# Masked softmax on one core: small writes to the output placed beside the first whole loads

## The chip, the cores and the metric

The kernel runs on one core of a Trainium2 chip. The metric is the device time of one execution in microseconds (us). The kernel before takes 156.7 us.

## The reference

```python
x: (16, 8, 256, 256) float32;  lengths: (16,) int32, 128 to 255
for b in range(16):
    length = lengths[b]
    m = x[b, :, :, :length]
    m = exp(m - max(m, axis=-1))
    result[b, :, :, :length] = m / sum(m, axis=-1)      # the rest of the row is 0
```

## The kernel before

Each of the 16 batch entries is one tile of 2 MB: 128 partitions, 16 rows of 256 floats each. SP's queue loads the first four tiles whole (the first in two halves) and later stores all sixteen. GpSimd loads the other twelve, only as wide as the length requires ("gap loads" in the prediction). VectorE masks a tile, ScalarE takes Exp row by row with the row sum, VectorE divides, SP stores. The output of the last tile is written at the very end.

```python
nc.scalar.dma_start(out=word64, in_=lengths[None, :]).then_inc(s_word, 16)
for h in range(2):                                     # tile 0 in two halves
    s = slice(h * half, (h + 1) * half)
    nc.sync.dma_start(out=xt[:, 0, s], in_=x_f[0, :, s]).then_inc(s_ld[h], 16)
for b in range(1, ahead):                              # tiles 1 to 3, whole
    nc.sync.dma_start(out=xt[:, b], in_=x_f[b]).then_inc(s_ld[b + 1], 16)
for b in range(batch):                                 # all stores
    for s in parts(b):
        nc.sync.wait_ge(s_out, 2 * b + (s.stop - 1) // half + 1)
        ...
        nc.sync.dma_start(out=out_f[b, :, s, :], in_=xt[:, b % slots, s, :]).then_inc(s_b, ...)
...
nc.gpsimd.wait_ge(s_ld[ahead - 1], 16)                 # GpSimd's loads begin after tile 2
with nc.Fori(0, (batch - ahead) // 2, 1, engines=[POOL]) as q:
    ...                                                # one narrow load for each later tile
...
nc.scalar.activation(out=warm, ...)                    # loads the Exp table
with nc.Fori(0, 2 * batch, 1, engines=[ACT]) as i:     # 8 Exp with row sums per half tile
    nc.scalar.wait_ge(s_min, i + 1)
    ...
```

The softmax here doesn't subtract the row's maximum and nothing guards it: scores larger than these inputs give would overflow.

Of the kernel before, what the change touches and what calls it, by code (L numbers as in the profile page):

```python
# [9 lines left out]
F32 = mybir.dt.float32  # L10
# [10 lines left out]
def kernel(  # L21
# [6 lines left out]
    nc = tc.nc  # L28
    P = nc.NUM_PARTITIONS

    batch, heads, seq_q, seq_k = x.shape
# [7 lines left out]
    out_f = out.rearrange("b h q k -> b (h q) k").rearrange("b (p t) k -> b p t k", p=P)  # L39
# [10 lines left out]
    def parts(b):  # L50


        if b == 0:
            cuts = [0, nt]
        elif b < 10:
            cuts = [0, half, half + quarter, nt]
        elif b < 12 or b == batch - 1:
            cuts = [0, half, nt]
        else:
            cuts = [0, nt]  # L60
        return [slice(i, j) for i, j in zip(cuts, cuts[1:])]

    pool = ctx.enter_context(tc.tile_pool(name="all", bufs=1))
# [10 lines left out]
    row_sum = pool.tile([P, batch, nt], F32, name="row_sum")  # L74
    inv_sum = pool.tile([P, batch, nt], F32, name="inv_sum")
    warm = pool.tile([P, 1], F32, name="warm")
    seed = pool.tile([1, 2], F32, name="seed")

    with tc.tile_critical(no_gpsimd_drain=True):  # L79
        sem = lambda n: ctx.enter_context(nc.semaphore(n))  # L80
        s_word = sem("s_word")
        s_ones = sem("s_ones")
        s_lenb = sem("s_lenb")
        s_lenf = sem("s_lenf")
        s_ld = [sem(f"s_ld{k}") for k in range(ahead + 1)]
# [18 lines left out]


        nc.scalar.dma_start(out=word64, in_=lengths[None, :]).then_inc(s_word, 16)
        for h in range(2):
            s = slice(h * half, (h + 1) * half)
            nc.sync.dma_start(out=xt[:, 0, s], in_=x_f[0, :, s]).then_inc(s_ld[h], 16)  # L109
        for b in range(1, ahead):  # L110
            nc.sync.dma_start(out=xt[:, b], in_=x_f[b]).then_inc(s_ld[b + 1], 16)  # L111
        for b in range(batch):
            s_b = s_st[b % 2]
            for s in parts(b):
                nc.sync.wait_ge(s_out, 2 * b + (s.stop - 1) // half + 1)
                if b >= 2 and s.start == 0:
                    nc.sync.wait_ge(s_b, 64 * (b // 2 + 1))
                nc.sync.dma_start(  # L118
                    out=out_f[b, :, s, :], in_=xt[:, b % slots, s, :]
                ).then_inc(s_b, 16 * ((s.stop - s.start) // quarter))  # L120
# [49 lines left out]
        def step(ins):  # L170
# [8 lines left out]
                out=down, in0=iota_i, scalar1=0.5, scalar2=-big, op0=ALU.add, op1=ALU.mult  # L179
# [7 lines left out]
                out=len_s, in0=len_f, scalar1=big, scalar2=None, op0=ALU.mult  # L187
# [56 lines left out]
        with nc.Fori(0, 2 * batch, 1, engines=[ACT]) as i:  # L244
            nc.scalar.wait_ge(s_min, i + 1)
            at = bass.ds(i % (2 * slots), 1)
            for j in range(half):
                e = x_h[:, at, j, :]
                ins = nc.scalar.activation(  # L249
                    out=e, in_=e, func=EXP, accum_out=sum_h[:, bass.ds(i, 1), j]  # L250
# [32 lines left out]
```

## Time and profile before

| | before |
|---|---|
| device time | 156.71 us median (156.7 to 157.01, 3 runs) |
| span in the profile | 154.7 us |
| busiest compute engine | VectorE, 115.1 us |
| queue shares of the DMA engines | 66.1% + 32.1% |
| stretch with a low rate | 20 to 24 us |

The span ends when the last store has landed. As the DMA engines are busy for nearly all of it, a change in this kernel is worth what it adds to or takes from their time. The prediction shows the lines and reads them.

The trace also has one record for each DMA packet, with its queue, size, start and duration. The usual duration of a packet, from the medians that the prediction gives, is 7 ns plus its bytes at 27.1 bytes per ns. A packet is called slow when it took over 1.25 times that. The "excess" of a stretch is the slow packets' time above the usual, of SP's and ScalarE's large packets (4 KB and more), summed and divided by 16 engines. By this count the kernel before has 0.96 us of excess from 19 to 24 us, and 0.60 us in the first 5 us; in the rest of the execution it has 0.03 us. (The prediction summed over all packets of the first stretch, not only the slow ones, and so has 1.1 us.)

### The profile page before, as it was taken

What the parts mean: (1) busy time and instruction counts of PE and PEld (TensorE: products, weight loads), DVE (VectorE), ACT (ScalarE), POOL (GpSimd) and SP (SyncE); (2) the same over time, 40 slices, a digit from 0 to 9 for tenths busy, and PEclk for the clock granted to TensorE, in tenths of its full rate; (3) what the DMA queues carried; (4) which work ended last, traced back from release to release, by engine and by line L of the source; (5) the groups of instructions that cost most, each with busy time, mean ns of one, the idle gap of its engine ahead of it and who ended that gap; (6) DMA issues with size and microseconds to landing.
All of it is one profiled execution on the core that took longest, in us unless ns stands there. A gap on an engine that the chain in (4) does not pass through costs nothing.

```text
span 154.7 us, 1317 instructions
## 1 busy us (share of the span) xinstructions
PE 0.2 (0%) x1; PEld 0.1 (0%) x1; DVE 115.1 (74%) x84; ACT 105.2 (68%) x514; POOL 19.0 (12%) x25
## 2 busy tenths in 40 slices
PE   0000000000000000000000000000000000000000
PEld 0000000000000000000000000000000000000000
DVE  1249999952999994966979499999894999990000
ACT  3087799992698997591978849798969297920000
POOL 4910031000320200202020020202000000000000
DMA  4999999999999999999999999999999999999993
GB/s 108 430 445 424 436 309 416 409 411 436 423 404 388 423 405 416 412 412 422 398 421 412 411 413 404 414 409 412 417 409 450 417 420 426 443 432 436 424 415 144
DMA packets 10132, 62.08 MB, mean 401 GB/s; under 512 B 866, under 2 KB 962, under 8 KB 6802
## 3 DMA queue, kind: packets, MB, share of 16 engines
q1 hardware_dynamic: 6048, 41.95, 66.1%
q0 software_dynamic: 4080, 20.12, 32.1%
q14 instruction: 2, 0.02, 0.0%
q10 hardware_dynamic: 2, 0.00, 0.0%
HBM read 28.51 MB, written 33.55 MB: 401 GB/s over the span
## 4 chain that ended last, share of the span: by engine, by line
DMA 71%; DVE 12%; issue 4%; POOLq 1%; SPq 1%; DVEq 0%
DMA xt<-in_x_dram 60%; DMA out_dram<-xt 11%; DVE xt L222 9%; DVE xt L195 3%; SPq L109 1%; POOLq L135 1%; DVE inv_sum L219 0%; POOLq L130 0%; SPq L111 0%; SPq L118 0%; POOLq L157 0%; POOLq L159 0%; DVEq L212 0%; POOLq L137 0%; SPq L278 0%
## 5 line engine op out<-in xcount | busy, mean ns | idle before, releaser
L249 ACT ACTIVATE xt<-xt x256 | 102.4, 402 | 29.6 <-DVE xt L195 29.6
L222 DVE TENSOR_TENSOR xt<-xt,inv_sum 128x2048 f32<-128x2048 f32 x32 | 73.3, 2292 | 1.1
L195 DVE SCALAR_TENSOR_TENSOR xt<-down,len_s,xt 128x2048 f32<-128x2048 f32 (+1 forms) x17 | 37.8, 2224 | 19.8 <-DMA xt<-in_x_dram 19.4
L249 ACT ACTIVATION_READ_ACCUMULATOR xt<-xt x256 | 48.1, 188 | 0.0
L130 POOL DMA_DIRECT2D xt<-in_x_dram x12 | 12.8, 1066 | 91.3 <-DMA out_dram<-xt 62.8
L219 DVE RECIPROCAL inv_sum<-row_sum 128x8 f32<-128x8 f32 x32 | 6.3, 196 | 1.2 <-ACT xt L249 1.2
L149 POOL MEMSET xt<- 128x1536 f32 x4 | 5.3, 1387 | 1.1 <-DVE len_s L186 1.1
L241 ACT ACT_TABLE_LOAD x1 | 1.3, 1283 | 1.6 <-SPq L79 1.6
L178 DVE TENSOR_SCALAR down<-iota_i 128x256 f32<-128x256 int32 x1 | 0.3, 299 | 1.6 <-POOL iota_i L141 1.6
L183 DVE CAST len_b<-word 1x16 bf16<-1x16 int32 x1 | 0.2, 162 | 0.4 <-DMA word<-in_lengths_dram 0.4
L186 DVE TENSOR_SCALAR len_s<-len_f 128x16 f32<-128x16 f32 x1 | 0.2, 175 | 0.3 <-PE len_f L165 0.3
L141 POOL IOTA iota_i<- 128x256 int32 x1 | 0.3, 332 | 0.6 <-SPq L79 0.6
L146 POOL MEMSET seed<- 1x1 f32 x2 | 0.3, 164 | 0.0
L241 ACT ACTIVATE warm<-const-float32-0.0 128x1 f32<-128x1 f32 x1 | 0.2, 203 | 0.0
L144 POOL MEMSET ones<- 1x128 bf16 x1 | 0.2, 197 | 0.0
L165 PE MATMUL len_f<-len_b,ones 1*128 1x16 bf16 x1 | 0.2, 164 | 2.6 <-DVE len_b L183 2.6
L267 POOL MEMSET const-float32-0.0<- 128x1 f32 x1 | 0.1, 99 | 0.3 <-issue 0.3
L165 PEld LDWEIGHTS len_f<-len_b,ones 1*128 1x128 bf16 x1 | 0.1, 99 | 2.6 <-POOL ones L144 2.6
L267 POOL MEMSET const-float32-1.0<- 128x1 f32 x1 | 0.1, 99 | 0.0
L267 POOL MEMSET const-bfloat16-1.0<- 128x1 bf16 x1 | 0.1, 99 | 0.0
L267 POOL MEMSET const-uint8-127<- 128x1 uint8 x1 | 0.1, 99 | 0.0
L267 POOL BASE_LOAD x1 | 0.0, 17 | 0.1
## 6 DMA issues: line engine op xcount, KB each, us to landing
out_dram<-xt SPq DMA_DIRECT2D x15, 1024.0 KB
out_dram<-xt SPq DMA_DIRECT2D x18, 512.0 KB
out_dram<-xt SPq DMA_DIRECT2D x4, 2048.0 KB
xt<-in_x_dram SPq DMA_DIRECT2D x3, 2048.0 KB, 16.1
xt<-in_x_dram POOLq DMA_DIRECT2D x3, 1728.0 KB, 15.9
xt<-in_x_dram POOLq DMA_DIRECT2D x2, 2048.0 KB, 17.5
xt<-in_x_dram POOLq DMA_DIRECT2D x2, 1600.0 KB, 15.1
xt<-in_x_dram POOLq DMA_DIRECT2D x2, 1280.0 KB, 14.2
```

The lines of the kernel that those rows point to most:

```text
L109: nc.sync.dma_start(out=xt[:, 0, s], in_=x_f[0, :, s]).then_inc(s_ld[h], 16)
L130: nc.gpsimd.dma_start(out=xt[:, slot, :, :w], in_=x_n[:, n, :, :w]).then_inc(s_sw[par], 16)
L135: with nc.gpsimd.If(v <= ws[m]):
L141: nc.gpsimd.iota(iota_i, pattern=[[1, seq_k]], base=0, channel_multiplier=0).then_inc(s_iota, 1)
L149: nc.gpsimd.memset(xt[:, b, :, low:], 0.0).then_inc(s_fill, 1)
L165: nc.tensor.matmul(len_f, lhsT=ones, rhs=len_b, start=True, stop=True).then_inc(s_lenf, 1)
L195: return nc.vector.scalar_tensor_tensor(out=t, in0=down[:, None, lo:hi].to_broadcast([P, s.stop - s.start, hi - lo]), scalar=len_s[:, b : ...
L219: step(nc.vector.reciprocal(out=inv_sum[:, b, s], in_=row_sum[:, b, s]))
L222: nc.vector.tensor_tensor(out=t, in0=t, in1=inv_sum[:, b, s, None].to_broadcast([P, half, seq_k]), op=ALU.mult,).then_inc(s_out, 1)
L241: nc.scalar.activation(out=warm, in_=nc.const_aps.tensor(0.0, (P, 1), F32), func=EXP)
L249: ins = nc.scalar.activation(out=e, in_=e, func=EXP, accum_out=sum_h[:, bass.ds(i, 1), j])
L267: nc = _bacc.Bacc("TRN2", target_bir_lowering=False, num_devices=1)
```

## The change

The change wants to start writing early. While the whole loads run, ScalarE's queue writes zeros to the place of the last tile in the output, 40 pieces of 64 bytes ("touches" from here on) by each of the 16 DMA engines. The real store of that tile writes over them at the end, after a wait that keeps the two in order.

```diff
+    few = 16
+    often = 40
+    touch = pool.tile([16, often, few], F32, name="touch")
...
+        nc.vector.memset(touch, 0.0).then_inc(s_zero, 1)
+        nc.scalar.wait_ge(s_zero, 1)
+        out_e = out_f[batch - 1].rearrange("(e r) t k -> e (r t) k", e=16)[:, :often, :few]
+        nc.scalar.dma_start(out=out_e, in_=touch).then_inc(s_touch, 16)
...
+                if b == batch - 1 and s.start == 0:
+                    nc.sync.wait_ge(s_touch, 16)
```

(The two new semaphores are cut.)

More of the change, by code (lines that the diff above doesn't have):

```diff
@@ L82 @@
         s_ones = sem("s_ones")
+        s_touch = sem("s_touch")
+        s_zero = sem("s_zero")
         s_lenb = sem("s_lenb")
```

## The prediction

> **What bounds the kernel now.** I read the page from the top: busy shares first, then the slices, the DMA queues and the chain, and last the windows of the stretch that the change enters.
>
> The page's engine shares, slices and queue table:
>
> ```profile
> PE 0.2 (0%) x1; PEld 0.1 (0%) x1; DVE 115.1 (74%) x84; ACT 105.2 (68%) x514; POOL 19.0 (12%) x25
> ...
> DMA  4999999999999999999999999999999999999993
> GB/s 108 430 445 424 436 309 416 409 411 436 423 404 388 423 405 416 412 412 422 398 421 412 411 413 404 414 409 412 417 409 450 417 420 426 443 432 436 424 415 144
> DMA packets 10132, 62.08 MB, mean 401 GB/s; under 512 B 866, under 2 KB 962, under 8 KB 6802
> ...
> q1 hardware_dynamic: 6048, 41.95, 66.1%
> q0 software_dynamic: 4080, 20.12, 32.1%
> q14 instruction: 2, 0.02, 0.0%
> q10 hardware_dynamic: 2, 0.00, 0.0%
> ```
>
> No compute engine is over 74%, while the DMA row is 9 from the second slice to the last but one. The queue shares add up to 98.2% of 16 engines over 154.7 us, that is 152 us of transfer per DMA engine. The chain says the same:
>
> ```profile
> DMA 71%; DVE 12%; issue 4%; POOLq 1%; SPq 1%; DVEq 0%
> DMA xt<-in_x_dram 60%; DMA out_dram<-xt 11%; DVE xt L222 9%; DVE xt L195 3%; SPq L109 1%; POOLq L135 1%; DVE inv_sum L219 0%; POOLq L130 0%; SPq L111 0%; SPq L118 0%; POOLq L157 0%; POOLq L159 0%; DVEq L212 0%; POOLq L137 0%; SPq L278 0%
> ```
>
> So the kernel lasts as long as 16 saturated DMA engines need: 62.08 MB at some 413 to 432 GB/s, plus 2.5 us before the first bytes flow and about 2.5 us of completion at the end. The one real hole is slice six (309 GB/s). The windows around it (length in us, busy time of PE, PEld, DVE, ACT, POOL, then clock, DMA share, GB/s):
>
> ```profile
> 2.00:3.00 1.00, 0.16 (x1) 0.10 (x1) 0.34 (x2) 0.99 (x2) 0.00 (x0) 1.00 0.88 164
> 3.00:4.00 1.00, 0.00 (x0) 0.00 (x0) 0.00 (x0) 0.14 (x1) 0.96 (x1) 1.00 0.87 319
> 4.00:8.00 4.00, 0.00 (x0) 0.00 (x0) 1.28 (x1) 0.00 (x0) 4.00 (x4) 1.00 1.04 440
> 8.00:19.00 11.00, 0.00 (x0) 0.00 (x0) 8.62 (x7) 8.97 (x45) 0.38 (x1) 1.00 1.01 432
> 19.00:20.00 1.00, 0.00 (x0) 0.00 (x0) 1.00 (x1) 1.00 (x6) 0.00 (x0) 1.00 1.02 410
> 20.00:21.00 1.00, 0.00 (x0) 0.00 (x0) 1.00 (x1) 1.00 (x7) 0.15 (x1) 1.00 1.20 393
> 21.00:22.00 1.00, 0.00 (x0) 0.00 (x0) 0.96 (x3) 1.00 (x6) 1.00 (x1) 1.00 1.12 262
> 22.00:23.00 1.00, 0.00 (x0) 0.00 (x0) 1.00 (x1) 1.00 (x7) 0.14 (x1) 1.00 0.58 197
> 23.00:24.00 1.00, 0.00 (x0) 0.00 (x0) 0.97 (x3) 1.00 (x6) 0.41 (x1) 1.00 0.96 361
> 24.00:26.00 2.00, 0.00 (x0) 0.00 (x0) 2.00 (x2) 2.00 (x11) 0.15 (x1) 1.00 1.03 438
> ```
>
> From 19 to 24 us the five windows move 1623 units (GB/s times us) where 5 x 432 = 2160 would be normal: 537 / 432 = 1.2 us lost. The trace's packet records put it on the last whole load and the first packets of the first store. A 16 KB packet of that queue usually takes 611 ns; 94 of them in this stretch are up to 1354 ns, and their excess, divided by 16 engines, is 1.1 us. The first store is issued at 18.75 us, the dip begins an engine queue's length later, and no later passage from loads to stores shows anything like it. It is therefore a cost of the first stores, or at least coincides with them. The change writes to the output before that, among the whole loads, in many tiny pieces; I take its intent to be to wake up writing early and take this hole away.
>
> **What the Trainium skill says.** "DMA: Bandwidth & Descriptors", section "Queues, rings and completion order": a DMA engine takes turns between the queues that have work, a packet at a time. No row of before shows two queues during the first 20 us, but later q0 and q1 share the engines at 413 GB/s (26 to 90 us), so turning costs little there. The same page, "Specifications": below 512 B a transfer isn't at line rate, because of a read-modify-write. The trace before has no small write to HBM to test that with; its 864 packets of 4 B (9 ns each) are semaphore updates, and its one 128 B load packet took 11 ns. The same page, "Why small descriptors are slow (HBM only)": about 3 cycles of overhead per packet over 32 B a cycle. The packet records agree for large ones: 162 ns for 4 KB, 309 for 8 KB, 611 for 16 KB, which is 27 bytes per ns and some 7 to 10 ns fixed. "Trainium Kernel Development and Optimization", section "Key Constraints": queues of SP, ACT and POOL all run on the same 16 DMA engines. So the new queue buys no bandwidth; its packets come out of the same engine time.
>
> **The change part by part.** Nothing is removed.
>
> One VectorE memset of 16 partitions x 640 floats. From the 128x256 tensor_scalar (299 ns) and the 128x1024 mask (1.28 us), about 1.1 to 1.2 ns per element and partition: at most 0.75 us, from about 1.0 us on. VectorE's first instruction stood at 1.61 us, so that is late by perhaps 0.2 us; the first thing that matters on VectorE is the mask at 6.60 us, behind a load. Path: 0.
>
> A wait and one more DMA on ScalarE's sequencer, with 640 rows of 64 B, 40 for each DMA engine. An issue took 0.52 us (lengths, 2 packets) and 0.42 to 0.69 us (whole loads, 144 packets). If it grew fully with the number of rows it would be 3 us: 1.7 + 3 = 4.7, table load 1.28, warm-up 0.2, ends at 6.2 us. The first Exp starts at 8.15 us, so ScalarE has about 2 us to spare. Path: 0. SP's three whole-load issues (2.05 to 3.88 us) could be held up by it, but the first 2 MB feed the engines until about 7.3 us. Path: 0.
>
> 640 packets of 64 B and 16 semaphore packets among the loads. Per engine there are 16 packets of 8 KB and 24 of 16 KB in the whole loads, 40 in all: taking turns, one touch goes between each two. By the records a touch should cost 7 to 10 ns fixed and 2.4 ns for its bytes, about 10 ns; 41 x 10 ns = 0.4 us per engine. If a small write to HBM costs something like 50 ns (my estimate for read-modify-write: five times the bare packet), 41 x 50 = 2.05 us. All of this is on the path: the first store still has work queued until about 29 us (its last semaphore packet is at 30.1 us) when the next store (issued 26.08 us) and the first gap loads (first packet 26.07 us) come in, so there is no idle time that absorbs it, and 98% busy engines afterwards carry it to the end.
>
> The dip. If the early writes pay for whatever the first stores wait for, up to 1.1 us goes from 20 to 24 us; part of it may reappear at 3 to 5 us, where the records already show 0.6 us of excess in the first load packets. The engines are full from 24 us on, so a gain here would reach the end too.
>
> A wait on SP before the last tile's first store: long fulfilled, under 0.1 us on a sequencer with deep queues behind it. Path: 0. Extra bytes: 640 x 64 B = 41 KB of 62 MB, 0.1 us at full rate, contained above.
>
> Sum, central: touches +0.4 to +0.8, dip -0.3 on average over my doubt: about +0.3 us, hence 157.0 us.
>
> **Rivals.** (a) The hole closes: -1.1 + 0.4 = -0.7, about 156.0 us. For it: the hole is there once only, just when writing begins. Against: the slow packets are load packets in front of the store, and the touched addresses are in the last tile, not in the first. (b) The hole stays and the touches cost bare packets: +0.4, 157.1. For it: a small write elsewhere changes nothing for the first store's own rows. (c) Every small write is slow (50 ns or more) and stops the load behind it: +2, 158.7; at 100 ns +4, 160.8. For it: the skill's 512 B sentence and 40 turnings per engine. Against: 9 to 11 ns for the tiny packets that there are. (d) ScalarE or the queues' issuing is held up beyond 8 us, so that Exp of tile 0 starts late: the first store has some 4 us of spare time, so even that would be hardly seen.
>
> **Range and chances.** Weights: (a) 0.3, (b) 0.4, (c) 0.25 with a tail to 161, (d) 0.05. The middle lies near 157.0, with 8 in 10 between 155.8 and 159.0. Faster by over 2% needs under 153.6, three times the hole: 0.02. Slower by over 2% needs over 159.8, that is touches of 80 ns or a stall per touch: 0.09. The rest, 0.89, is within 2%.
>
> **What would show it.** Queue q10 must rise from 2 to 658 packets with a share of some 0.2 to 1.3%; its mean packet time is the disputed cost. The windows of 20 to 24 us show whether the hole closes; those of 2 to 8 us whether it merely moved. The landing of the whole loads (median 16.1 us) should move by the touches' cost. The first Exp must stay near 8.2 us. I am wrong if q10's packets take over 80 ns, if DMA has a new idle stretch before 24 us, or if ScalarE's first Exp is late by over 4 us.

## The result, and the profile after

The changed kernel takes 156.49 us (156.45 to 156.68, 4 runs), beside 156.74 us (156.7 to 157.01, 4 runs) of the kernel before. The ratio is 0.9983, with a 95% interval of 0.9965 to 1.0. A ratio here is the mean time of one kernel's runs over that of the other's of the same rounds, so it is not quite the ratio of the two medians. Six more runs gave the other sign, 1.0026, so the 0.25 us of the first set isn't a gain to explain.

The page after, its rates, packets and queues:

```profile
GB/s 110 425 442 421 425 353 405 405 412 439 418 406 390 417 407 421 410 413 415 405 424 407 411 419 401 415 406 413 416 411 448 417 423 425 442 436 428 425 417 127
...
q1 hardware_dynamic: 6048, 41.95, 65.9%
...
q10 hardware_dynamic: 658, 0.04, 0.3%
...
HBM read 28.51 MB, written 33.60 MB: 401 GB/s over the span
```

ScalarE's queue, q10, now has 656 packets more (640 touches and 16 semaphore updates), and they take 0.3% of the engines. That is 0.44 us for each engine, 11 ns for one touch. The page's HBM line adds the touches to what is written and nothing to what is read. That is no test for a reading inside a small write: the bytes read (28,508,288 in every run here) are exactly the sum of the program's load packets, so the line is an account of the transfers and not a measurement at the memory. The sixth slice of the rates is still a hole, 353 GB/s where it was 309.

The chain of work that ended last, by engine and by line:

```profile
DMA 71%; DVE 12%; issue 3%; SPq 2%; POOLq 1%; DVEq 0%
DMA xt<-in_x_dram 39%; DMA out_dram<-xt 32%; DVE xt L235 9%; DVE xt L208 3%; SPq L131 1%; SPq L120 1%; DVE inv_sum L232 0%; POOLq L104 0%; POOLq L143 0%; SPq L122 0%; POOLq L148 0%; POOLq L166 0%; DVEq L225 0%; POOLq L170 0%; POOLq L150 0%
```

Transfers are 71% of it in both kernels. That it now runs more through stores (32%, before 11%) and less through loads (39%, before 60%) shows only that, where both queues are full, either can be the one that is followed back.

The instructions at the start, in order of time (start and duration in us, engine, line, operation; a q behind the engine's name is its sequencer issuing a transfer):

```profile
1.32 0.59 DVE L114 MEMSET touch<- 16x640 f32 x1 [1.32 <-SPq L82]
...
1.95 0.41 ACTq L117 DMA_DIRECT2D out_dram<-touch  x1
...
2.39 1.28 ACT L254 ACT_TABLE_LOAD   x1 [2.39 <-DVE touch L114]
...
8.01 0.42 ACT L262 ACTIVATE xt<-xt  x1 [4.12 <-DVE xt L208]
```

The memset takes 0.59 us. The issue of 640 pieces takes 0.41 us, less than the 0.54 us for the lengths. The table load ends at 3.67 us, and the first Exp starts at 8.01 us, behind the mask, as before (8.15 us).

The windows in which the kernel before had its hole (length, busy time of PE, PEld, DVE, ACT, POOL, then clock, DMA share, GB/s):

```profile
20.00:21.00 1.00, 0.00 (x0) 0.00 (x0) 1.00 (x1) 1.00 (x7) 0.20 (x1) 1.00 1.20 428
21.00:22.00 1.00, 0.00 (x0) 0.00 (x0) 0.97 (x3) 1.00 (x6) 1.00 (x1) 1.00 1.46 378
22.00:23.00 1.00, 0.00 (x0) 0.00 (x0) 1.00 (x1) 1.00 (x7) 0.10 (x1) 1.00 0.54 197
23.00:24.00 1.00, 0.00 (x0) 0.00 (x0) 0.96 (x3) 1.00 (x6) 0.27 (x1) 1.00 0.93 346
24.00:26.00 2.00, 0.00 (x0) 0.00 (x0) 2.00 (x2) 2.00 (x12) 0.29 (x1) 1.00 0.93 391
```

The hole is there as before. From 20 to 26 us the six microseconds move 428 + 378 + 197 + 346 + 2 x 391 = 2131, and before 393 + 262 + 197 + 361 + 2 x 438 = 2089, a difference of 0.1 us at 432 GB/s. The excess of slow packets is 0.78 us, before 0.96 us.

The packet records show the touches at work. The first starts at 5.83 us, 3.5 us after its issue ended, when an engine has begun some 9 packets of the first tile. From there one touch follows each large packet: from 9 to 12 us, 76 large packets and 76 touches. By 20.9 us an engine has done some 30 of its 40 and the whole loads are nearly over; the last touch starts at 29.2 us, among the stores. So the engines did write to HBM, in turns with the loads, for 14 us before the hole came, and it came all the same.

### The profile page after: what moved, and what is told of

The parts are those of the page before. It is cut to its first block, busy times and chain, and to the rows that moved or that the text cites. A ratio compares the mean times of both kernels' runs of the same rounds, so it can differ in the third digit from the quotient of the medians.

```text
span 154.8 us, 1319 instructions
## 1 busy us (share of the span) xinstructions
PE 0.2 (0%) x1; PEld 0.1 (0%) x1; DVE 115.6 (75%) x85; ACT 105.2 (68%) x514; POOL 19.0 (12%) x25
## 4 chain that ended last, share of the span: by engine, by line
DMA 71%; DVE 12%; issue 3%; SPq 2%; POOLq 1%; DVEq 0%
DMA xt<-in_x_dram 39%; DMA out_dram<-xt 32%; DVE xt L235 9%; DVE xt L208 3%; SPq L131 1%; SPq L120 1%; DVE inv_sum L232 0%; POOLq L104 0%; POOLq L143 0%; SPq L122 0%; POOLq L148 0%; POOLq L166 0%; DVEq L225 0%; POOLq L170 0%; POOLq L150 0%
## 5 line engine op out<-in xcount | busy, mean ns | idle before, releaser
L114 DVE MEMSET touch<- 16x640 f32 x1 | 0.6, 592 | 1.3 <-SPq L82 1.3
```

The source lines that it names most:

```text
L114: nc.vector.memset(touch, 0.0).then_inc(s_zero, 1)
```

## The experiments

The first question was what a touch costs and whether the 0.25 us is real; the second was what the hole is, if early small writes don't close it.

### The same kernel again

No edit.

> The changed kernel once more, with more rounds, to say whether its 0.25 us (ratio 0.9983, interval 0.9965 to 1.0) is there at all. Theory A (the touches cost their bare packet time, 0.44 us per DMA engine, and the hole at 20 to 24 us merely fills in a little): ratio 0.998 to 1.003, hole still there at 20 to 24 us. Rival B (the touches do take a real cost from the first stores): ratio 0.9965 to 0.9985 with an interval that stays under 1.

Measured: 157.15 us (6 runs) beside 156.83 us of the kernel before (11 runs), ratio 1.0026, interval 1.0002 to 1.005. Excess 0.83 us from 19 to 24 us, and 11 ns a touch. This excludes rival B's range: the sign turned. Both ratios are within 0.3% of 1 and both intervals within 0.5%, on either side: 40 touches change the time by no more than that.

### 80 touches for each engine

```diff
-    often = 40
+    often = 80
```

> The changed kernel with 80 touches per DMA engine in place of 40: 1280 packets of 64 B. If their engine time (11 ns each as recorded) lies on the path, 40 more add 0.44 us: ratio about 0.003 above the run with 40, so 1.000 to 1.002. If small packets are nearly free because they slip in beside the large ones, the ratio is within 0.001 of the run with 40. If each one holds up the large packet behind it by 50 ns, 2 us more: ratio 1.011. The touches should then still be running at about 40 us, one per large packet of the queue of SP.

Measured: 157.12 us, ratio 1.0024 (1.0 to 1.0049), 0.0002 below the run with 40. Still 11 ns each, 0.88 us for an engine; the last one starts at 47.9 us, one per turn. A cost of 50 ns for each is out. By its letter the expectation would call this "nearly free", but between that and "on the path" the spread of the runs doesn't decide.

### 240 touches for each engine

```diff
-    often = 40
+    often = 120
...
+        for j in range(2):
+            out_e = (the same rows, columns j * few to (j + 1) * few)
+            nc.scalar.dma_start(out=out_e, in_=touch).then_inc(s_touch, 16)
-                    nc.sync.wait_ge(s_touch, 16)
+                    nc.sync.wait_ge(s_touch, 32)
```

> The changed kernel with 240 touches per DMA engine (two transfers of 120 rows each), six times as many, to see a cost that 40 and 80 leave in the noise. If 11 ns each are engine time on the path: 240 x 11 ns = 2.64 us over the kernel before, ratio 1.015 to 1.019. If they slip in beside the large packets: ratio 1.000 to 1.004. They should then be under way until 80 to 120 us, one per turn.

Measured: 160.3 us, ratio 1.0229 (1.0207 to 1.0252). This is outside both ranges, and for a reason that neither had. The start of ScalarE, in order of time:

```profile
3.28 17.63 ACTq L120 DMA_DIRECT2D out_dram<-touch  x2
...
20.94 1.28 ACT L257 ACT_TABLE_LOAD   x1 [20.94 <-issue]
...
22.34 0.40 ACT L265 ACTIVATE xt<-xt  x1
```

The second issue did not end until 20.94 us, when only about 26 of the 240 touches of an engine had run. ScalarE stood behind it, and the first Exp started at 22.34 us in place of 8.15 us. The touches were not under way until 80 us or later, either: the last one started at 25.4 us, and some 3300 of all 3840 ran from 22 to 25 us, when little else was ready. The run tells nothing about the cost of a touch on the path. It does tell two other things. Rival (d) of the prediction, ScalarE held up by an issue, is real at six times the size. And with the first store held back to 32.9 us the hole at 20 us is gone:

```profile
20.00:21.00 1.00, 0.00 (x0) 0.00 (x0) 0.00 (x0) 0.06 (x1) 0.06 (x1) 1.00 1.05 444
21.00:22.00 1.00, 0.00 (x0) 0.00 (x0) 0.00 (x0) 1.00 (x1) 1.00 (x1) 1.00 0.97 411
```

No load packet of this stretch is slow (they take 611 ns), although GpSimd's first load was issued at 20.94 us as usual. In their place 0.41 us of excess stands at 36 to 40 us, among the first store's packets, and another 0.95 us, which the count leaves out, on GpSimd's load packets at 40 to 44 us. So it looks put off and not saved. Here it came some 2 us behind the store's first packets (34 us) and not ahead of them; this run changes too much else to say why.

### 120 touches for each engine

```diff
-    often = 40
+    often = 120
```

> The changed kernel with 120 touches per DMA engine in one transfer, the most that earlier runs took in one issue without holding ScalarE. Theory A (each touch's 11 ns is engine time on the path): 80 more than in the change, 0.9 us more, ratio to the kernel before 1.006 to 1.009. Rival (a touch slips in beside the large packets): 1.001 to 1.004, as with 40 and 80. ScalarE's issue stays near 0.4 us, so that its first Exp stays near 8.3 us.

Measured: 157.38 us, ratio 1.0048 (1.0026 to 1.007). The issue took 0.37 us and the first Exp started at 8.18 us, so ScalarE is out of it here. The touches took 1.32 us of each engine, 0.84% of the time; the interval ends below that. It lies across the gap between the two ranges, so this run doesn't decide cleanly either. The sum of all packets of an engine rises by 1.07 us, from 151.87 us in the profile of before to 152.94 us, and the last packet ends 0.93 us later (153.72 and 152.79 us). That looks like the touches' time on the path, but it doesn't show it. Two variants below without any touch end nearly as late: 153.57 us with the whole loads on ScalarE's queue, where the sum is 151.92 us, and 153.67 us with the first store in two halves. Nor do the ratios of the small variants go by the number of touches: 1.0009 and 1.0027 with none, 1.0024 with one, 1.0025 with 16, 1.0026 with 40, 1.0024 with 80. Beside the 1.0027 of the half store, from the same rounds, 120 touches add 0.2%. Whether the touches' engine time ends up on the path stays open.

### GpSimd's first load later

```diff
-        nc.gpsimd.wait_ge(s_ld[ahead - 1], 16)
+        nc.gpsimd.wait_ge(s_ld[ahead], 16)
```

> The kernel before, with GpSimd's first gap load waiting for the last whole load (landed about 24.5 us) and not for the one before it (18.6 us); so the first descriptor writing by GpSimd moves from 20.8 us to about 25 us or later. Theory C (the hole at 20 to 23 us is the first gap load's issue on GpSimd): the windows 20 to 23 us come to over 400 GB/s and a hole of about 1.1 us appears some 4 us later. Theory D (the hole is the first store entering the queue behind the loads): the hole stays at 20 to 23 us. Time: 156 to 159 us, as the engines have work until about 29 us.

Measured: 157.49 us, ratio 1.0044 (1.0015 to 1.0073). GpSimd's first load was issued at 27.22 us instead of 20.84 us. The hole did not move with it:

```profile
21.00:22.00 1.00, 0.00 (x0) 0.00 (x0) 0.96 (x3) 1.00 (x7) 0.00 (x0) 1.00 1.21 311
22.00:23.00 1.00, 0.00 (x0) 0.00 (x0) 1.00 (x1) 1.00 (x6) 0.00 (x0) 1.00 0.69 229
23.00:24.00 1.00, 0.00 (x0) 0.00 (x0) 0.97 (x3) 1.00 (x7) 0.00 (x0) 1.00 1.01 426
```

GpSimd does nothing here, and the rate still drops to 311 and 229 GB/s. Theory C falls. (This run has a second slow stretch, from 48 to 51 us: GpSimd's load packets of 4.7 KB take 267 ns there in place of 194 ns, almost all alike, while hardly a store runs. It may be why the run is slower; no run here explains it.)

### The first store later

```diff
+                if b == 0:
+                    nc.sync.wait_ge(s_ld[ahead], 16)
```

> The kernel before, with the first store held until the last whole load has landed (about 23.5 us if nothing slows it). Theory D (the hole is the first store entering the queue): the windows 20 to 22 us stay over 400 GB/s, the last whole load lands about 1 us earlier, and slow packets come with the store. Theory C (GpSimd's first gap load, issued at 20.8 us): the hole stays at 20 to 23 us. In both there is a new idle stretch of about 2 us between the last load and the first store's bytes: 158 to 160 us.

Measured: 158.51 us, ratio 1.0113 (1.0082 to 1.0143). From 19 to 24 us not one of SP's packets is slow, and the last engine's semaphore packet for the last whole load is at 23.18 us in place of 24.34 us. So the hole does belong to the first store. Holding the store back is no way to save it:

```profile
20.00:21.00 1.00, 0.00 (x0) 0.00 (x0) 1.00 (x1) 1.00 (x6) 0.01 (x1) 1.00 0.80 344
21.00:22.00 1.00, 0.00 (x0) 0.00 (x0) 0.97 (x3) 1.00 (x7) 1.00 (x1) 1.00 1.15 492
22.00:23.00 1.00, 0.00 (x0) 0.00 (x0) 1.00 (x1) 1.00 (x6) 0.28 (x1) 1.00 0.24 98
23.00:24.00 1.00, 0.00 (x0) 0.00 (x0) 0.97 (x3) 1.00 (x7) 0.56 (x1) 1.00 0.99 171
...
26.00:27.00 1.00, 0.00 (x0) 0.00 (x0) 1.00 (x2) 1.00 (x6) 0.00 (x0) 1.00 1.21 269
27.00:28.00 1.00, 0.00 (x0) 0.00 (x0) 1.00 (x1) 1.00 (x7) 0.00 (x0) 1.00 0.82 225
```

From 20 to 22 us the mean is 418 GB/s (344 and 492: a single window scatters with the starts of the 16 KB packets). From 22 to 23 us the engines wait for work; their share is 0.24. Then the hole is back. The store's first packet starts at 27.73 us, and from 26 to 28 us 38 of GpSimd's load packets are slow, up to 972 ns where 191 ns are usual, 0.79 us of excess; shares and rates look like those of the hole before. So theory D's third sign, slow packets with the store, is there: the hole moved with the store, from SP's load packets to GpSimd's, which the count of the other sections leaves out. (Another 0.77 us of slow GpSimd packets stands at 23 to 26 us, where that queue begins. It is not explained; in the kernel before that queue begins at 26.07 us without any.)

### The whole loads on ScalarE's queue

```diff
-        nc.scalar.dma_start(out=word64, ...)
+        nc.sync.dma_start(out=word64, ...)
-            nc.sync.dma_start(out=xt[:, 0, s], ...)
+            nc.scalar.dma_start(out=xt[:, 0, s], ...)
-            nc.sync.dma_start(out=xt[:, b], in_=x_f[b])...
+            nc.scalar.dma_start(out=xt[:, b], in_=x_f[b])...
```

> The kernel before with the five whole-load issues on ScalarE's queue (and the lengths on SP's), so that no queue has stores behind whole loads. Theory D2 (load packets run slow when a store follows them in the same queue; the hole is that one passage, since later the queue of SP has only stores): no packet over 1.25 times its usual duration from 19 to 24 us, windows 20 to 23 us over 400 GB/s, the last whole load shares turns with the first store; up to 1 us faster, ratio 0.993 to 0.998. Theory D3 (it is the first large write, whatever the queue): slow packets at 19 to 22 us as before, ratio 0.999 to 1.003.

Measured: 156.97 us, ratio 1.0009 (0.9989 to 1.0028). The hole stays, with 0.93 us of excess, and it still lies on the load packets, which are now alone in their queue. Theory D2 falls: it doesn't take one queue. The store was issued at 18.67 us and its first packet starts at 23.16 us, so it shared turns with the last load (whose last packet starts at 24.03 us) for less than 1 us: it waited 4.5 us, as the touches had waited 3.5 us.

### One touch for each engine in SP's own queue

```diff
-        nc.scalar.dma_start(out=out_e, in_=touch).then_inc(s_touch, 16)
...
             nc.sync.dma_start(out=xt[:, b], in_=x_f[b]).then_inc(s_ld[b + 1], 16)
+            if b == 1:
+                nc.sync.wait_ge(s_zero, 1)
+                nc.sync.dma_start(out=out_e, in_=touch).then_inc(s_touch, 16)
```

(With one piece for each engine, and without ScalarE's wait.)

> One touch per DMA engine (16 packets of 64 B), on SP's own queue, between the second and the third whole load, none on ScalarE's queue. Theory D2 (a write that follows loads in the same queue slows the load packets ahead of it): slow load packets appear ahead of it, at 9 to 12.5 us, with up to 1 us of excess, and the hole at 20 to 23 us stays. Rival (only large stores do this): no slow packets before 19 us. Time: ratio 1.000 to 1.007.

Measured: 157.07 us, ratio 1.0024 (1.0002 to 1.0046). From 9 to 19 us no packet is slow; the touches pass between 12 and 14 us. This fits the rival's "only large stores do this", against D2. The hole at 20 to 24 us stays, though smaller in this one profile (0.40 us). The time did not gain by it.

### 16 touches into the first tile's place

```diff
-    often = 40
+    often = 16
...
-        out_e = out_f[batch - 1].rearrange(...)
+        out_e = out_f[0].rearrange(...)
...
-                if b == batch - 1 and s.start == 0:
+                if b == 0 and s.start == 0:
                     nc.sync.wait_ge(s_touch, 16)
```

> 16 touches per DMA engine into the first tile's place in the output instead of 40 into the last, landed before the first store. If the hole is the first write to those addresses, it closes: no slow packets at 20 to 23 us, ratio 0.993 to 0.998. If the place is of no account, the hole stays with 0.8 to 1.1 us of excess and the ratio is 0.998 to 1.003.

Measured: 156.99 us, ratio 1.0025 (1.0001 to 1.005). The last touch starts at 13.5 us, well before the store; the hole stays with 0.80 us of excess. Touching the very tile that is stored first does not help. (Only the first rows of each engine's share of it were touched, so "the same addresses" holds for the tile and not for every row.)

### An early write of 1 MB

```diff
-    touch = pool.tile([16, often, few], F32, name="touch")
+    touch = pool.tile([128, half, seq_k], F32, name="touch")
...
-        nc.vector.memset(touch, 0.0).then_inc(s_zero, 1)
...
-        nc.scalar.dma_start(out=out_e, in_=touch)...
+        nc.scalar.dma_start(out=out_f[batch - 1, :128, :half], in_=touch)...
...
+        nc.gpsimd.memset(touch, 0.0).then_inc(s_zero, 1)
```

> In place of the touches one early write of 1 MB of zeros (8 packets of 8 KB per DMA engine, 8 x 309 ns = 2.5 us) into the last tile's place, from ScalarE's queue at about 4 us. Theory E (the hole is paid once, by the first large write): slow load packets move to the time when that write enters, 5 to 9 us, and the windows 20 to 24 us come to over 400 GB/s; ratio about 1.013 to 1.018. Theory F (each time a large write enters among whole loads): slow packets in both places; ratio 1.016 to 1.024.

Measured: 158.96 us, ratio 1.0149 (1.0132 to 1.0166). This one moves the hole. The windows of 5 to 8 us and of 20 to 24 us:

```profile
5.00:6.00 1.00, 0.00 (x0) 0.00 (x0) 0.00 (x0) 0.47 (x2) 1.00 (x2) 1.00 1.04 393
6.00:7.00 1.00, 0.00 (x0) 0.00 (x0) 0.52 (x1) 0.00 (x0) 1.00 (x2) 1.00 1.16 328
7.00:8.00 1.00, 0.00 (x0) 0.00 (x0) 0.77 (x1) 0.00 (x0) 1.00 (x2) 1.00 0.81 246
...
20.00:21.00 1.00, 0.00 (x0) 0.00 (x0) 1.00 (x1) 1.00 (x7) 0.00 (x0) 1.00 0.92 393
21.00:22.00 1.00, 0.00 (x0) 0.00 (x0) 0.92 (x2) 1.00 (x6) 0.00 (x0) 1.00 0.96 410
22.00:23.00 1.00, 0.00 (x0) 0.00 (x0) 1.00 (x1) 1.00 (x7) 0.00 (x0) 1.00 1.18 508
23.00:24.00 1.00, 0.00 (x0) 0.00 (x0) 1.00 (x1) 1.00 (x6) 0.00 (x0) 1.00 0.84 360
```

Now 0.75 us of excess lies from 5 to 9 us, on load packets, mostly ahead of the early write's own packets, of which the first come between 7 and 8 us. From 19 to 24 us there is none, and when the first real store passes, about 28 to 31 us, only 0.04 us; of GpSimd's packets one is slow in the whole run. This fits theory E, and not F: here the cost is paid once, by the first large write. The write itself took 2.47 us of each engine (its row of the packet records), and the time rose by 0.0149 x 156.65 = 2.3 us; moving the hole gained nothing to speak of.

### An early write of 128 KB

The same with 16 partitions, one packet of 8 KB for each engine.

> The same with one 8 KB packet per DMA engine (128 KB, 0.3 us). If theory E holds and the size of a packet is what matters, the hole moves here too, and as 0.3 us of work then stand against a hole of about 1 us, which may overlap with the start, the ratio is 0.995 to 1.002. If one packet is not enough, the hole stays at 20 to 24 us: 1.001 to 1.004.

Measured: 156.94 us, ratio 1.0016 (0.9998 to 1.0035). The hole stays with 0.82 us of excess; the stretch where the early packet came in has 0.06 us. One large packet for each engine is not enough, eight are (by one profile each).

### The first store in two halves, from 14 us on

```diff
         if b == 0:
-            cuts = [0, nt]
+            cuts = [0, half, nt]
```

> The kernel before with the first tile stored in two halves, so that the first store is issued at about 14 us and not at 18.75 us, still behind the whole loads in the queue of SP. Theory G (the load packets run slow from some 2 us after the store's issue): slow packets at 15 to 18 us. Theory H (the last packets of the last load run slow, because the store comes right behind them): slow packets stay at 20 to 23 us. Time in both: ratio 0.998 to 1.003.

Measured: 157.19 us, ratio 1.0027 (1.0003 to 1.0052). The first store was issued at 14.44 us, 4 us earlier, but behind the same loads in SP's queue. The windows:

```profile
20.00:21.00 1.00, 0.00 (x0) 0.00 (x0) 1.00 (x1) 1.00 (x7) 0.00 (x0) 1.00 1.12 377
21.00:22.00 1.00, 0.00 (x0) 0.00 (x0) 0.97 (x3) 1.00 (x6) 0.75 (x1) 1.00 1.32 295
22.00:23.00 1.00, 0.00 (x0) 0.00 (x0) 1.00 (x1) 1.00 (x7) 0.54 (x1) 1.00 0.52 164
```

No packet is slow from 9 to 19 us, and 1.09 us of excess stands at 20 to 24 us. The slow packets are tied to the approach of the store's own packets (the first starts at 23.30 us), up to 3.5 us ahead of them, and not to its issue: theory H, not G. Of the 46 slow packets 10 are the store's own.

## Why the prediction was right

The predicted 157.0 us and its range (155.8 to 159.0 us) hold both sets of runs, 156.49 and 157.15 us. The number by itself proves little: the range spans 3.2 us and holds rivals (a) and (b) both, and the first set's 156.49 us lies about midway between their 156.0 and 157.1 us. That it fell so near to 157.0 us is in part luck; which rival is right only the traces tell. Step by step:

- **What bounds the kernel** held. The DMA engines stay the bound, and ScalarE, VectorE and SP have room for the additions: the memset took 0.59 us (at most 0.75 predicted), the issue 0.41 us (the fear was 3 us), and the first Exp stayed put.
- **The cost of a touch** was put at 10 ns and is 11 ns: 0.44 us an engine with 40 of them, where the sum said 0.4. The rival of a slow small write (50 ns or more) is refuted by the packet durations at 40, 80 and 120 touches. One reading behind it was wrong: the large packets were said to agree with 3 cycles of overhead over 32 B a cycle. At their 27 bytes per ns 32 B take 1.2 ns and 3 cycles 3.5 ns, half of the 7 ns that they show; the 10 ns came out right because they were taken from the records and not from that figure. (The prediction's 94 packets from 19 to 24 us are 99 by our count, with the same 1.1 us.)
- **Taking turns**, one touch between two large packets, held once it had begun. The prediction supposed that it would begin at once. It began 3.5 us after the issue and so ended at 29.2 us, after the whole loads instead of with them. The landing of the whole loads, which was to move by the touches' cost, hardly did: the median is 16.0 us, before 16.1 us. That median is the load of tile 2, which ends at 18.2 us in both profiles, before the hole, so a smaller hole is not the reason. Taken over all 16 engines its semaphore packets are later by 0.17 us on average (17.87 and 17.70 us), where 25 touches of an engine had taken 0.28 us.
- **All of it is on the path** is not shown. With 40 and 80 touches the runs scatter by more than that. With 120 the time rose by 0.48%, and the interval ends at 0.70%, below the 0.84% of the touches alone, so not all of it showed at the end; and variants without touches also lie up to 0.27% above the kernel before.
- **The dip.** Rival (a), that the early writes close the hole, had a weight of 0.3 and fell. Rival (b), that it stays and the touches cost their bare packets, is what happened. The guess behind the central sum, 0.3 us of the hole saved on average, has no run to rest on: the excess goes from 0.96 to 0.78 and 0.83 us, within its scatter over the other variants with a hole (0.40 to 1.09 us). Naming the hole a cost of the first stores was right: a store that is held back takes the hole along, and when GpSimd's load is held back the hole stays. What the prediction did not foresee is that small writes don't count for it, neither in the last tile nor in the first, and that it takes a large write, of 8 packets an engine and not of one, to bring it forward.

What the slow load packets are waiting for while the first large write approaches stays open. The runs rule out GpSimd's first load, the sharing of a queue, the issue's own time and the mere fact of a first write to HBM; they don't show a mechanism. No variant beats the kernel before by more than the scatter, and there is little to be had: the whole hole is about 1 us, 0.6%, and paying it earlier costs the same.

## What to carry to other kernels

A hole in the DMA rate is an invitation, but before one fills it one asks what has to be true for the remedy to act on it; here one run with the suspected transfer held back, and one with the other suspect held back, settled whose hole it was. The count has to take in every queue: with GpSimd's left out, the hole of the held-back store seemed to have vanished. Small writes among large transfers are cheap (11 ns each in this kernel) and also do little: what the first bulk store costs, it costs when the first bulk store comes. When a variant is built to magnify a cost, one checks in its timeline that it is the same cost: six times the touches stopped ScalarE for 17 us and measured something else.

## What the Trainium skill lacked or had wrong

- "DMA: Bandwidth & Descriptors", "Specifications", says that below 512 B a transfer is not at line rate because of a read-modify-write. The rate part agrees (64 B in 11 ns is 5.8 bytes per ns, 16 KB packets run at 26.8). A reading shows no time of its own: a write of 64 B takes as long as the read of 128 B (11 ns) and 2 ns more than a semaphore update of 4 B. Whether it takes place, no run here shows.
- The same page, "Queues, rings and completion order", says that an engine takes turns between queues packet by packet. This holds in steady state (76 large packets and 76 touches from 9 to 12 us). It has a whole packet at each turn, typically 9 to 17 descriptors; no such group of touches shows here, where they and the large packets of the trace are equal in number. It lacks that a queue filled while the engines are busy waits first: 3.3 to 3.9 us from the end of the issue to the first packet in the runs with early writes, 4.5 us from the issue of the first store in its own queue to its first packet.
- No page gives how much one issue can hold before the sequencer stands: 80 and 120 pieces for each engine were issued in 0.37 us, a second 120 behind the first held ScalarE for 17 us. "Perfetto Trace Analysis" names a descriptor buffer that can be full, without a size.
- No page has the cost that comes with the first large write: 0.4 to 1.1 us of excess, mostly on load packets ahead of it, put off when it is held back (0.79 us at 26 to 28 us, on GpSimd's packets), brought forward by a write of 8 packets of 8 KB for each engine (0.75 us at 5 to 9 us), not by one of them, nor by 64 B writes.
